# Two encoder layers on one core: measured costs in the planner that places the mixers' steps, a third MLA head at a time, and a different first group

## The chip, the cores and the metric

One core of a Trainium2 chip runs the whole kernel in one launch. The metric is device time in microseconds: the median over several runs, beside one profiled execution from which all rows come. The engines are PE (TensorE), ACT (ScalarE), DVE (VectorE), POOL (GpSimd) and SP (SyncE), which here only issues DMAs.

## The reference, cut to what matters

Two layers, 256 tokens, width 2048, all in float32. Each layer is

```python
h = rms_norm(x, norm_mix)
z = h @ w_in                       # 2048 -> 4304 columns, split over three mixers
y = concat(mlstm(...), mla(...), dilated(...))   # 4, 6 and 6 heads of 128
x = x + y @ w_out
h = rms_norm(x, norm_ff)
x = x + relu(h @ w_ff1) ** 2 @ w_ff2             # 2048 -> 8192 -> 2048
```

The MLA heads (latent attention) take their queries, keys and values from two normed latents of the first columns of z; the dilated heads are attention with a bias of window counts; the mLSTM heads are two directions of a gated linear attention.

## The kernel before, in words

**Products.** A float32 product is three products of float32r parts: hi x hi, hi x lo, lo x hi. Every weight tile (128 x 1024, two contraction tiles of 512 columns) is loaded by SP into one of three buffers `wst`, cast to `whi` by ACT, and DVE takes the rest into `wlo` (`Weights.load`, `split`); four pairs of `whi` and `wlo` exist, and three are made ahead. In the text a unit is one weight tile and its twelve products of 512 columns, w0, w1, ... are the weight tiles in order, and g in a row is the PSUM of such products. Two PSUM banks take a group, one for each tile of 128 tokens, and four banks (`gps`) serve all groups.

**Stages.** A layer's mixers run nine groups of eight units: group 0 (the MLA latents), group 1 (336 columns: key's rotary part, gates, part of dilated v), groups 2 to 4 (mLSTM q and k, v, output gate), 5 to 8 (dilated). Between them come MLA heads, each with a weight tile of its own (`mla_z`), at the places `MLA_AT` = (group, unit). Then come the output projection and four chunks of feed-forward.

**Order.** The program is written by a planner at build time (`Stream`): the main line issues the products, and every evacuation, head or norm is a task, a generator, of which a step is issued when its due time comes. The planner's clock advances by the cost of each product (`mm`), the due time of a step by the cost of what it waits for on ACT, DVE and POOL (`Engine.COST`) plus `MARGIN`. PE takes its instructions in that order, so a step written too early is a wait of PE. `Stream.start` holds back the main line until there is room: a head needs two PSUM banks (`m`), three `t2` tiles and three `half` tiles; while it is held back, steps of other tasks are issued with no products between them. `junk`, `ss` and `xss` are squares and their sums; `nk`, `nkT`, `qrT`, `mla_s`, `sm_e`, `pT`, `oT` are the stations of an MLA head in this order (normed q and k, transposed, rotary part transposed, scores, softmax, transposed, output); `ml_w`, `ml_st`, `ml_h`, `ml_yT` are an mLSTM head's.

**First group.** In the first layer x comes transposed (`xT`, eight loads). `first_xg` splits it on ACT and DVE, and POOL squares it into `acc`, of which two `stat` products make the mean; `token_factor` makes the token factor `rt` of it. x itself (two loads of 1 MB) is loaded after group 1 (`after()`). The latents, `z` and `dv` are read out of PSUM with `rt`.

Of the kernel before, what the change touches and what calls it, by code (L numbers as in the profile page):

```python
# [17 lines left out]
P = 128  # L18
# [48 lines left out]
T2, HALF = 22, 7  # L67

MLA_AT = ((2, 3), (2, 7), (3, 3), (3, 7), (4, 3), (4, 7))
MARGIN = 0.4  # L70


class Engine:
# [3 lines left out]
        "activation": (0.16, 0.00083), "copy": (0.07, 0.00083), "tensor_tensor": (0.07, 0.00104),  # L77
        "scalar_tensor_tensor": (0.13, 0.00104), "tensor_scalar": (0.07, 0.00080), "tensor_copy": (0.07, 0.00104),
        "tensor_reduce": (0.07, 0.00104), "tensor_tensor_reduce": (0.07, 0.00104), "reciprocal": (0.07, 0.0066),
        "tensor_tensor_scan": (0.07, 0.00104), "memset": (0.07, 0.0004),  # L80
    }

# [3 lines left out]
    def __getattr__(self, f):  # L86
# [4 lines left out]
        def call(*args, **kw):  # L91
# [25 lines left out]
class Stream:  # L117
# [98 lines left out]
class Weights:  # L216
# [7 lines left out]
    def load(self):  # L224
# [3 lines left out]
        c.nc.sync.dma_start(self.st[self.d][:, :n], src)  # L228
        self.d += 1

    def split(self):

        c, nc = self.c, self.c.nc
        st, n = self.st.pop(self.k), self.srcs[self.k][1]
# [3 lines left out]
        def parts():  # L238
            nc.scalar.copy(hi[:, :n], st[:, :n])
            yield  # L240
            nc.vector.tensor_tensor(out=lo[:, :n], in0=st[:, :n], in1=hi[:, :n].bitcast(F32), op=ALU.subtract)
# [94 lines left out]
def first_xg(c, xg, kt, src, gain):  # L336
# [11 lines left out]
    c.s.cur.last.pop("pool", None)  # L348
# [987 lines left out]
```

## Time and profile before

| what | us |
|---|---|
| median of 3 runs (2155.4 to 2157.72) | 2156.25 |
| the profiled execution | 2155.49 |
| its span, first to last instruction | 2153.3 |
| PE busy in it | 2119.8 |
| DVE, ACT, POOL busy | 1322.4, 1082.3, 110.4 |

The span lies 2.2 us below the profiled execution's own time. Busy time of PE is modelled at its ends, so a short wait shows shorter than it is.

### The profile page before, as it was taken

How to read it: one execution, taken by the hardware profiler on the slowest of the kernel's cores; microseconds unless marked ns; L12 is line 12 of the kernel's file. 1: busy time of each engine (PE TensorE's matmuls, PEld its weight loads, DVE VectorE, ACT ScalarE, POOL GpSimd, SP SyncE). 2: the span in 40 equal slices, each digit the busy share in tenths (PEclk: the TensorE clock that was granted, in tenths of full speed). 3: DMA queues.
4: the chain of work that ended last, by engine and by line, in shares of the span. 5: the costliest groups of instructions: out<-in, count | busy, mean ns of one | idle time of the engine just before them, and what ended most of it. 6: DMA issues, size and time to landing. Idle time of an engine off the chain costs nothing.

```text
span 2153.3 us, 28894 instructions
## 1 busy us (share of the span) xinstructions
PE 2119.8 (98%) x10848; PEld 1804.9 (84%) x10848; DVE 1322.4 (61%) x1963; ACT 1082.3 (50%) x1883; POOL 110.4 (5%) x142
## 2 busy tenths in 40 slices
PE   8999999999999999999999999999999999999999
PEld 6788888888888888888887888888888888888887
DVE  7668755655564565565557687556546655655654
ACT  5666655543453444454456676554434434534442
POOL 6112100000000000000001121000000000000000
PEclk9999999999999999999999999999999999999999
DMA  7544455566656666566554444556565666566565
GB/s 228 189 141 126 154 175 181 187 194 190 193 186 195 194 188 193 190 192 196 178 174 142 143 128 153 174 189 192 186 198 189 190 191 195 187 195 194 187 200 162
DMA packets 109004, 389.89 MB, mean 181 GB/s; under 512 B 12352, under 2 KB 12480, under 8 KB 108608
## 3 DMA queue, kind: packets, MB, share of 16 engines
q1 hardware_dynamic: 107136, 384.97, 56.6%
q10 hardware_dynamic: 1728, 3.07, 0.4%
q8 instruction: 85, 1.39, 0.3%
q14 instruction: 55, 0.45, 0.1%
HBM read 385.90 MB, written 2.10 MB: 180 GB/s over the span
## 4 chain that ended last, share of the span: by engine, by line
PE 89%; ACT 4%; DVE 3%; POOL 2%; issue 1%; DMA 1%; POOLq 0%; ACTq 0%; DVEq 0%; SPq 0%
PE g L194 84%; ACT junk L98 1%; PE mla_z L194 1%; ACT whi L98 1%; DVE wlo L98 1%; POOL acc L98 1%; PE oT L194 1%; POOL sq L98 1%; DMA wst<-w_in 1%; PE xT L200 0%; PE pT L200 0%; PE dil_s L194 0%; PE mla_s L194 0%; POOL rp L98 0%; ACT dil_z L98 0%
## 5 line engine op out<-in xcount | busy, mean ns | idle before, releaser
L98 DVE TENSOR_TENSOR wlo<-wst,whi 128x1024 fp32r<-128x1024 f32 (+2 forms) x732 | 889.5, 1224 | 317.4 <-ACT whi L98 307.7
L98 ACT CAST whi<-wst 128x1024 fp32r<-128x1024 f32 (+2 forms) x732 | 761.2, 1043 | 539.7 <-PE g L194 402.5
L194 PE MATMUL g<-whi,u 128*128 128x512 f32 x2048 | 633.4, 389 | 0.0
L194 PE MATMUL g<-xg,whi 128*128 128x512 f32 x2048 | 489.8, 391 | 0.0
L194 PEld LDWEIGHTS g<-whi,u 128*128 128x128 f32 x2048 | 384.5, 188 | 79.6
L194 PEld LDWEIGHTS g<-xg,whi 128*128 128x128 f32 x2048 | 376.4, 188 | 72.8
L194 PE MATMUL g<-wlo,u 128*128 128x512 f32 x1024 | 398.4, 389 | 0.0
L194 PE MATMUL g<-whi,xg 128*128 128x512 f32 (+1 forms) x1152 | 371.7, 389 | 6.3 <-ACT whi L98 6.3
L194 PEld LDWEIGHTS g<-xg,wlo 128*128 128x128 f32 x2048 | 263.1, 191 | 12.1 <-ACT xg L98 2.0
L194 PE MATMUL g<-xg,wlo 128*128 128x256 f32 x2048 | 267.4, 283 | 1.1 <-ACT xg L98 1.1
L194 PEld LDWEIGHTS g<-whi,xg 128*128 128x128 f32 x1152 | 215.5, 189 | 44.0 <-ACT whi L98 6.3
L194 PEld LDWEIGHTS g<-wlo,u 128*128 128x128 f32 x1024 | 192.3, 188 | 39.8
L194 PE MATMUL g<-wlo,xg 128*128 128x512 f32 (+1 forms) x576 | 222.0, 385 | 3.3 <-DVE wlo L98 3.3
L98 ACT COPY ev<-g 128x256 f32<-128x256 f32 x128 | 48.0, 375 | 340.7 <-PE g L194 340.7
L98 DVE TENSOR_TENSOR ev<-g,ev 128x256 f32<-128x256 f32 x128 | 54.4, 425 | 229.8 <-ACT ev L98 229.7
L194 PE MATMUL g<-whi,y 128*128 128x512 f32 x512 | 162.8, 393 | 0.0
L194 PEld LDWEIGHTS g<-wlo,xg 128*128 128x128 f32 x576 | 109.1, 189 | 23.3 <-DVE wlo L98 6.7
L194 PEld LDWEIGHTS g<-whi,y 128*128 128x128 f32 x512 | 96.1, 188 | 19.7
L194 PE MATMUL g<-wlo,y 128*128 128x512 f32 x256 | 99.7, 389 | 0.0
L98 DVE SCALAR_TENSOR_TENSOR x<-g,r,x 128x512 f32<-128x512 f32 x64 | 45.8, 751 | 83.2 <-PE g L194 83.2
L98 DVE SCALAR_TENSOR_TENSOR ev<-ev 128x256 f32<-128x256 f32 x128 | 54.4, 425 | 4.4
L194 PEld LDWEIGHTS g<-wlo,y 128*128 128x128 f32 x256 | 48.1, 188 | 9.5
(206 smaller groups left out, 1199.1 us busy)
## 6 DMA issues: line engine op xcount, KB each, us to landing
wst<-w_ff SPq DMA_DIRECT2D x512, 512.0 KB, 4.2
wst<-w_in SPq DMA_DIRECT2D x128, 512.0 KB, 3.7
wst<-w_out SPq DMA_DIRECT2D x64, 512.0 KB, 4.2
wst<-w_in SPq DMA_DIRECT2D x16, 336.0 KB, 3.0
wst<-w_mla SPq DMA_DIRECT2D x12, 416.0 KB, 3.1
xt<-xT SPq DMA_DIRECT2D x8, 256.0 KB, 5.1
x<-x SPq DMA_DIRECT2D x2, 1024.0 KB, 7.1
out<-x ACTq DMA_DIRECT2D x8, 256.0 KB, 2.2
```

Of the source, the lines that this page charges most:

```text
L98: return fn(*args, **kw)
L194: c.nc.tensor.matmul(out, lhsT, rhs, start=start, stop=stop)
```

## The change

Six edits. (1) The planner's cost table gets other numbers: larger fixed parts, POOL at four times DVE's cost by element, an accumulating activation 0.2 more, an engine free 0.08 before an instruction's cost is over; a product of 512 columns counts 0.2266, not 0.2158. (2) `HALF` is 9, not 7, and MLA heads begin at other places. (3) At most two mLSTM heads run at once. (4) The first layer's token factor comes from x itself: eight squares on ACT (`squares`), as every other norm has it; POOL's squares, `acc` and the `stat` products are gone, and the two loads of x stand in the last two units of group 0. (5) Ten float32 products of ones, 128 x 128, stand ahead of everything (`warm_up`); the first `xT` load is on ACT's queue, and the first weight tile is loaded, cast and split in two halves. (6) The very last unit does its six products for the first token tile, then the six for the second.

```diff
-T2, HALF = 22, 7
-
-MLA_AT = ((2, 3), (2, 7), (3, 3), (3, 7), (4, 3), (4, 7))
+T2, HALF = 22, 9
+
+MLA_AT = ((2, 7), (3, 4), (4, 1), (4, 7), (5, 5), (6, 3))
 MARGIN = 0.4
+ML_AT_ONCE = 2
+WARM = 10
...
     COST = {
-        "activation": (0.16, 0.00083), "copy": (0.07, 0.00083), "tensor_tensor": (0.07, 0.00104),
+        "activation": (0.26, 0.00086), "copy": (0.19, 0.00084), "tensor_tensor": (0.155, 0.00105),
...
+    OVERLAP, READ = 0.08, 0.2
...
             if self.name == "pool":
-                fixed, each = 0.15, 2 * each
-            self.s.issue(self.name, fixed + each * n)
+                fixed, each = 0.3, 4 * each
+            elif self.name == "act" and kw.get("accum_out") is not None:
+                fixed += self.READ
+            self.s.issue(self.name, fixed + each * n, self.OVERLAP)
...
-    def issue(self, name, cost):
+    def issue(self, name, cost, overlap):
         last = self.cur.last
         t = max([self.free[name], self.clk] + [v for k, v in last.items() if k != name])
-        self.free[name] = t + cost
+        self.free[name] = t + cost - overlap
...
-    c.s.product(n / 2400.0 * (1 if lhsT.dtype == F32R else 4) + 0.0025)
+    c.s.product(n / 2400.0 + 0.0133 if lhsT.dtype == F32R else n / 1200.0 + 0.0025)
...
+    def pieces(self, i):
+
+        n = self.srcs[i][1]
+        return [slice(0, n // 2), slice(n // 2, n)] if i == 0 else [slice(0, n)]
...
-    if kt == 0:
-        c.acc = c.small.tile([P, S], F32, tag="acc", name="acc", bufs=1)
-        nc.gpsimd.tensor_tensor(out=c.acc, in0=src, in1=src, op=ALU.mult)
-    else:
-        sq = c.tmp.tile([P, S], F32, tag="sq", name="sq", bufs=1)
-        nc.gpsimd.tensor_tensor(out=sq, in0=src, in1=src, op=ALU.mult)
-        nc.gpsimd.tensor_tensor(out=c.acc, in0=c.acc, in1=sq, op=ALU.add)
...
+def squares(c, tt, g, ss):
+
+    j = c.tmp.tile([P, 512], F32, tag="junk5", name="junk5", bufs=1)
+    c.nc.scalar.activation(j, c.x[tt][:, g * 512:(g + 1) * 512], AF.Square, accum_out=ss[:, tt, g:g + 1])
...
+def last_unit(c, acts, ps, w):
+
+    hi, lo = c.w.next()
+    for tt in range(NT):
+        for j in range(2):
...
+    if first:
+        c.xss = new_ss(c)
         for tt in range(NT):
...
+            for g in range(NX):
+                squares(c, tt, g, c.xss)
+            yield
+    yield
+    mean_square(c, v, c.xss)
...
+def warm_up(c):
+
+    ones = c.big.tile([P, P], F32, tag="big", name="ones")
+    c.nc.vector.memset(ones, 1.0)
+    ps = new_bank(c, "warm")
+    for _ in range(WARM):
+        c.nc.tensor.matmul(ps[:, :P], ones, ones, start=True, stop=True)
...
 def ml_head(c, h):
     nc = c.nc
+    yield from c.s.take(t2=2, half=1, ml=1)
...
+        if kp >= KT // 2 - NT:
+            tt = kp - KT // 2 + NT
+            nc.sync.dma_start(c.x[tt], x[tt])
...
+    load_x(nc.scalar)
```

Where this moves instructions, as the two programs have them (line 98 of before is line 104 of the change, 194 is 200, 200 is 206).

First excerpt, ACT in the first layer from the last unit of group 0 on. `rs_a` and `rs_y` are the logarithm and exponent of the token factor, `lat` the latents' squares. Before:

```order
L98 CAST whi<-wst 128x1024 x2
L98 CAST whi<-wst 128x672 x3
L98 ACTIVATE rs_a<-tf_v 128x2
L98 ACTIVATE rs_y_408<-rs_a 128x2
L98 CAST whi<-wst 128x672
L98 ACTIVATE lat,lat_ss<-g,rt 128x384
L98 ACTIVATE lat,lat_ss<-g,rt 128x128
L98 ACTIVATE lat,lat_ss<-g,rt 128x384
L98 ACTIVATE lat,lat_ss<-g,rt 128x128
L98 CAST whi<-wst 128x672 x2
L98 ACTIVATE rs_a<-lat_ss 128x4
L98 ACTIVATE rs_y_476<-rs_a 128x4
```

In the change three casts of 672 columns, four squares of the first token tile, two casts, four squares of the second tile and three casts stand ahead of this piece:

```order
L104 ACTIVATE rs_a<-tf_v 128x2
L104 ACTIVATE rs_y_476<-rs_a 128x2
L104 CAST whi<-wst 128x1024
L104 ACTIVATE lat,lat_ss<-g,rt 128x384
L104 ACTIVATE lat,lat_ss<-g,rt 128x128
L104 ACTIVATE lat,lat_ss<-g,rt 128x384
L104 ACTIVATE lat,lat_ss<-g,rt 128x128
L104 CAST whi<-wst 128x1024
L104 ACTIVATE z_542<-g,rt 128x80 x2
L104 CAST whi<-wst 128x1024
L104 ACTIVATE junk,kr_ss<-z_542 128x64 x2
L104 ACTIVATE dv<-g,rt 128x256 x2
```

The token factor's two activations now come behind the squares and all eight casts of group 1. `z` and `dv`, whose reading gives the PSUM of group 1 free, follow after the latents' squares, and group 2's first product waits for `dv`'s part on DVE.

Second excerpt, PE at the third MLA head of the first layer (`mla_z` is its first product). Before:

```order
L194 MATMUL g<-wlo,xg 128x512
L194 MATMUL g<-whi,xg 128x512
L200 MATMUL nkT<-const,nk 128x128 x4
L200 MATMUL pT<-const,sm_e 128x128 x4
L200 MATMUL qrT<-const,qr 64x128 x2
L194 MATMUL oT<-p_hi,mla_vh 128x256
L194 MATMUL oT<-p_lo,mla_vh 128x256
L194 MATMUL oT<-p_hi,mla_vl 128x256
L194 MATMUL oT<-p_hi,mla_vh 128x256
L194 MATMUL oT<-p_lo,mla_vh 128x256
L194 MATMUL oT<-p_hi,mla_vl 128x256
L194 MATMUL mla_z<-whi,lat_hl 128x192
```

In the change:

```order
L200 MATMUL mla_s<-krh,qrT_sb 128x256
L200 MATMUL mla_s<-krl,qrT_sb 128x256
L200 MATMUL g<-whi,xg 128x512
L200 MATMUL g<-wlo,xg 128x512
L200 MATMUL g<-whi,xg 128x512
L200 MATMUL mla_z<-whi,lat_hl 128x192
L200 MATMUL mla_z<-wlo,lat_hl 128x192
```

Before, nkT of the second head, pT, qrT and oT of others stood without products ahead of the third head's mla_z. Now only three g products stand between another head's mla_s and it.

Third excerpt, PE in the change ahead of the fifth MLA head, in the sixth unit of group 5. Since the third head's mla_s PE has had 21 g products, two ml_h triples and the fourth head's nkT; behind the piece come three more oT, an ml_h triple and mla_z.

```order
L206 MATMUL qrT<-const,qr 64x128 x2
L206 MATMUL pT<-const,sm_e 128x128 x4
L200 MATMUL ml_h<-ml_va,ml_wt 128x129 x3
L200 MATMUL mla_s<-mla_k,mla_q 128x256 x3
L200 MATMUL mla_s<-krh,qrT_sb 128x256
L200 MATMUL mla_s<-krl,qrT_sb 128x256
L200 MATMUL mla_s<-mla_k,mla_q 128x256 x3
L200 MATMUL mla_s<-krh,qrT_sb 128x256
L200 MATMUL mla_s<-krl,qrT_sb 128x256
L200 MATMUL oT<-p_hi,mla_vh 128x256
L200 MATMUL oT<-p_lo,mla_vh 128x256
L200 MATMUL oT<-p_hi,mla_vl 128x256
```

Here, too, steps stand without g products between them: pT and oT of the third head, qrT and mla_s of the fourth. Before, the fifth head's mla_z stood at the end of the fourth unit of group 4.

On SP the first load of x stands behind w10, the second behind w11; before, both stood behind w19 and the first MLA weight.

## Rows read from the trace of the kernel before

**Rows 1.** The page's busy line: us and share of the span, instructions, by engine.

```profile
PE 2119.8 (98%) x10848; PEld 1804.9 (84%) x10848; DVE 1322.4 (61%) x1963; ACT 1082.3 (50%) x1883; POOL 110.4 (5%) x142
```

**Rows 2.** Stretches: length, busy us of each engine, granted clock, DMA share, GB/s.

```profile
6.00:12.00 6.00, 4.96 (x11) 3.59 (x12) 5.91 (x7) 4.82 (x10) 5.59 (x6) 1.00 1.00 372
...
52.00:75.00 23.00, 21.15 (x113) 17.36 (x114) 17.09 (x45) 12.98 (x35) 1.32 (x3) 1.00 0.67 237
75.00:300.00 225.00, 217.06 (x1167) 183.53 (x1166) 163.96 (x361) 148.57 (x405) 32.64 (x36) 0.98 0.46 145
95.00:110.00 15.00, 11.90 (x63) 9.94 (x63) 10.88 (x25) 10.06 (x32) 2.16 (x3) 0.77 0.31 91
300.00:600.00 300.00, 299.44 (x1518) 255.32 (x1517) 175.38 (x215) 140.81 (x188) 0.00 (x0) 1.00 0.60 189
1118.00:1361.00 243.00, 234.38 (x1274) 198.88 (x1274) 178.83 (x403) 161.23 (x442) 34.62 (x39) 0.99 0.46 145
```

**Rows 3.** Timeline of PE: start us, us, instruction, idle before it and its releaser.

```profile
6.34 0.80 PE L194 MATMUL g<-whi,xg 128*128 128x512 f32 x1 [6.34 <-ACT whi L98]
...
10.99 1.05 PE L194 MATMUL g<-whi,xg 128*128 128x512 f32 x2
...
15.10 0.62 PE L194 MATMUL g<-whi,xg 128*128 128x512 f32 x2
15.55 0.39 PE L194 MATMUL g<-wlo,xg 128*128 128x512 f32 x1
...
52.04 0.50 PE L194 MATMUL g<-wlo,xg 128*128 128x512 f32 x1 [0.52 <-DVE wlo L98]
```

**Rows 4.** PE's waits in 1118 to 1361: us in total, times, longest.

```profile
PE pT L200 <- DVE sm_e L98: 2.9, 1, 2.9
PE dqkT L200 <- POOL dil_z L98: 2.2, 2, 1.2
```

**Rows 5.** Timeline of PE at the third MLA head of the first layer.

```profile
96.79 0.28 PE L194 MATMUL mla_s<-krl,qrT_sb 128*128 128x256 f32 x1
...
101.83 1.17 PE L200 MATMUL pT<-const,sm_e 128*128 128x128 f32 x4 [2.46 <-DVE sm_e L98]
...
103.67 0.58 PE L194 MATMUL oT<-p_hi,mla_vh 128*128 128x256 f32 x1 [0.25 <-ACT p_hi L98]
```

**Rows 6.** Groups by shape, DVE and ACT, 60 to 2150: busy us, mean ns.

```profile
L98 DVE TENSOR_TENSOR wlo<-wst,whi 128x1024 fp32r<-128x1024 f32 x693 | 846.6, 1230 | 304.0 <-ACT whi L98 294.5
L98 ACT CAST whi<-wst 128x672 fp32r<-128x672 f32 x8 | 6.1, 758 | 9.6 <-PE g L194 5.7 <-DMA wst<-w_in 3.9
L98 ACT ACTIVATE junk<-x 128x512 f32<-128x512 f32 x24 | 15.1, 629 | 3.8 <-DVE x L98 3.4
```

**Rows 7.** Groups by shape, 0 to 36.

```profile
L98 DVE SCALAR_TENSOR_TENSOR xg<-xt,vec,xg 128x256 fp32r<-128x256 f32 x16 | 13.5, 886 | 4.6 <-ACT xg L98 4.6
L98 DVE TENSOR_TENSOR wlo<-wst,whi 128x1024 fp32r<-128x1024 f32 x8 | 13.3, 1671 | 0.1
```

**Rows 8.** PE's waits in 0 to 75.

```profile
PE g L194 <- DVE wlo L98: 2.7, 6, 0.8
PE ml_aT L200 <- DVE ml_na L98: 1.8, 1, 1.8
```

**Rows 9.** DMA issues, part 6 of the page: KB each, median us to landing.

```profile
x<-x SPq DMA_DIRECT2D x2, 1024.0 KB, 7.1
```

**Rows 10.** Timeline of ACT around group 1 and the loads of x.

```profile
39.01 0.58 ACT L98 ACTIVATE lat<-g,rt 128x384 f32<-128x384 f32 x1 [1.17 <-DVE rt L98]
...
40.73 0.21 ACT L98 ACTIVATION_READ_ACCUMULATOR lat<-g,rt 128x1 f32 x1
...
50.87 0.79 ACT L98 ACTIVATE z<-g,rt 128x80 f32<-128x80 f32 x2
...
63.88 1.05 ACT L98 CAST whi<-wst 128x1024 fp32r<-128x1024 f32 x1 [5.00 <-DMA wst<-w_in]
```

**Rows 11.** Timeline of DVE at the end of the run.

```profile
2148.61 1.43 DVE L98 SCALAR_TENSOR_TENSOR x<-g,r,x 128x512 f32<-128x512 f32 x2 [7.89 <-PE g L194]
```

More of the change, by code (lines that the diff above doesn't have):

```diff
@@ L238, in parts @@
         def parts():
-            nc.scalar.copy(hi[:, :n], st[:, :n])
+            for cols in pieces:
+                nc.scalar.copy(hi[:, cols], st[:, cols])
             yield
-            nc.vector.tensor_tensor(out=lo[:, :n], in0=st[:, :n], in1=hi[:, :n].bitcast(F32), op=ALU.subtract)
+            for cols in pieces:
+                nc.vector.tensor_tensor(out=lo[:, cols], in0=st[:, cols], in1=hi[:, cols].bitcast(F32),
+                                        op=ALU.subtract)
         t = c.s.spawn(parts())
@@ L358, in next_xg @@
     for tt in range(NT):
-        j = c.tmp.tile([P, 512], F32, tag="junk5", name="junk5", bufs=1)
-        nc.scalar.activation(j, c.x[tt][:, g * 512:(g + 1) * 512], AF.Square, accum_out=ss[:, tt, g:g + 1])
+        squares(c, tt, g, ss)
     for half in range(2):
@@ L430, in w_half, with token_factor @@
         part()
-def token_factor(c, rt):
+def token_factor(c, rt, first):
     nc = c.nc
     v = c.small.tile([P, 2], F32, tag="tf_v", name="tf_v")
-    if c.xss is None:
-        ps = yield from bank(c, "stat")
+    if first:
+        c.xss = new_ss(c)
         for tt in range(NT):
-            mm(c, ps[:, 2 * tt:2 * tt + 2], c.acc[:, tt * P:(tt + 1) * P], c.mean[:, :2], True, True)
-        yield
-        nc.vector.tensor_scalar(out=v, in0=ps[:, 0:4:2], scalar1=EPS, scalar2=None, op0=ALU.add)
-        c.s.give(m=1)
-    else:
-        yield
-        mean_square(c, v, c.xss)
+            for g in range(NX):
[3 more added lines that the diff above has]
+    mean_square(c, v, c.xss)
     y = yield from rsqrt(c, v, 2)
@@ L916, in ml_head @@
     nc = c.nc
+    yield from c.s.take(t2=2, half=1, ml=1)
     kk, qq, ql = c.mlqk[h]
-    yield from c.s.take(t2=2, half=1)
     ws = []
@@ L998, in ml_head, with mixers @@
     split(c, c.y[h], tp[:, :S])
-    c.s.give(m=1, t2=1, half=1)
-def mixers(c, prepare, after):
+    c.s.give(m=1, t2=1, half=1, ml=1)
+def mixers(c, prepare, first):
     nc, s = c.nc, c.s
@@ L1014, in mixers @@
     ps = in_group(c, 512, prepare=prepare)
-    tf = s.spawn(token_factor(c, rt))
+    tf = s.spawn(token_factor(c, rt, first))
     lat = s.spawn(latents(c, ps, rt, tf))
@@ L1024, in mixers @@
     s.spawn(ml_gates(c, z1))
-    if after:
-        after()
     def mla0():
@@ L1040, in mixers @@
     ps = in_group(c, 512, hooks(4))
-    og = s.spawn(ml_o(c, ps, rt))
+    s.spawn(ml_o(c, ps, rt))
     for h in range(ML_H):
@@ L1102, in ffn @@
             ps = two_banks(c)
-            token_group(c, us, ps, 512)
+            if last_layer and ch == NCHUNK - 1 and g == NX - 1:
+                token_group(c, us, ps, 512, range(KT // 2 - 1))
+                last_unit(c, us, ps, 512)
+            else:
+                token_group(c, us, ps, 512)
             c.s.spawn(ff2_end(c, ps, g, l, ch, last_layer, nxt))
@@ L1146, in encoder @@
     c = Ctx()
-    c.tc, c.s = tc, Stream(m=4, t2=T2, half=HALF, dil=4)
+    c.tc, c.s = tc, Stream(m=4, t2=T2, half=HALF, dil=4, ml=ML_AT_ONCE)
     c.nc = Engines(c.s, nc)
@@ L1168, in encoder @@
     c.w = Weights(c, weight_order(c, depth))
+    warm_up(c)
     rest = load_vectors(c, 0)
@@ L1201, in encoder @@
     cr = c.cp.tile([P, C_R], F32R, tag="const_r", name="const_rr")
-    for i in range(c.B_ST):
+    load_x(nc.scalar)
+    c.w.load()
+    for i in range(c.B_ST - 1):
         load_x()
@@ L1213, in encoder @@
     cc = lambda o: c.const[:, o:o + P]
-    c.ident, c.mean, c.one, c.triu, c.tril = cc(C_ID), cc(C_MEAN), cc(C_ONE), cc(C_TRIU), cc(C_TRIL)
+    c.ident, c.one, c.triu, c.tril = cc(C_ID), cc(C_ONE), cc(C_TRIU), cc(C_TRIL)
     c.dilb = c.const[:, C_DILB:C_DILB + NT * S].rearrange("p (t s) -> p t s", t=NT)
     c.identr, c.masks, c.sel = cr[:, 0:P], cr[:, P:3 * P], cr[:, 3 * P:3 * P + 64]
-    def load_tokens():
-        for tt in range(NT):
-            nc.sync.dma_start(c.x[tt], x[tt])
     for l in range(depth):
-        mixers(c, prepare if l == 0 else None, load_tokens if l == 0 else None)
+        mixers(c, prepare if l == 0 else None, l == 0)
         out_proj(c)
```

24 lines of the change are left out of this document (16 added, 8 removed).

## The prediction, made before the change had run

> **What bounds the kernel now.** I read the page's busy line first, then the busy time of each engine by stretches, then PE's waits in the stretches that have any, then the places themselves in the timeline.
>
> PE is busy for 2119.8 of 2153.3 us [rows 1], so at most some 33 us are idle, and the question is where. The stretches answer it [rows 2]. In 300 us of output projection and feed-forward PE misses 0.56 us: that kind of work, by far the longer part of the run, is bound by PE's own products, and no placing of steps can help it. In the mixers of the first layer (75 to 300) PE misses 225 - 217.06 = 7.9 us, in those of the second (1118 to 1361) 243 - 234.38 = 8.6 us. [...] So each layer's mixers lose about 8.3 + 3.4 = 11.7 us. The busy figure counts modelled ends, so I add 3 for short waits that it hides (an estimate: some 20 waits, and a product's record outlasts the distance to the next by 0.16, as two products are 0.45 from start to start but 0.62 to their end [rows 3]). The rest is at the start: the first product runs at 6.34, the third group's second one at 52.04 [rows 3].
>
> The biggest single wait of the mixers is pT's for sm_e, the next dqkT's for POOL [rows 4]. The timeline shows what the first is [rows 5]: the third MLA head is due in the stream and finds no room, since two heads hold 6 of 7 `half` tiles, and the first head's remaining steps are written out with no products between them. PE is through with mla_s at 97 and starts pT at 101.83, oT at 103.67. That is the stretch with clock 0.77.
>
> **The mixers.** Room for nine `half` tiles lets three heads run, and the new places put heads five or six units apart, not four. So the third head follows three products after another head's mla_s (second excerpt): its wait is gone. But two mLSTM heads now hold a `half` each when the fifth MLA head is due (third excerpt), 3 + 3 + 2 = 8 of 9, so that head must wait for the third to end, and steps stand there without products again. I walk it with the distances of [rows 5]. Before: mla_s to pT 4.9 us, pT to oT 1.8. Now PE has 21 g products of 0.225 [rows 3], 4.7 us, and besides two ml_h triples and nkT between mla_s and pT: that covers 4.9. Between pT and oT stand an ml_h triple and a whole mla_s (ten products of half the columns, 1.1): 1.6 to 1.8, just enough. But the softmax steps queue on DVE behind a reciprocal of ml_og and a wlo (1.23 [rows 6]), so I put 1.5 us of waiting there, and no fall of the clock. Bounds: 0, if all is covered; 13 as in rival 4. Saved: 3.1 idle (15 - 11.90 [rows 2]) + 3.4 clock - 1.5 = 5.0 us a layer.
>
> The other waits (11.7 - 6.5 = 5.2, with the hidden 3 about 8 us a layer) are steps that PE meets too early, as dqkT on POOL, 2.2 [rows 4]. The new table charges POOL four times DVE's cost by element, not twice, and the fixed parts of DVE and ACT at about twice the old; a product is charged 0.2266, near what the trace shows, not 0.2158. Steps of such chains therefore stand later. I take half of the 8, 4 us; bounds 1 (waits only change places, as DVE and ACT have the same work to do) and 6. No operation is added to the mixers, and DVE stays below PE (178.8 of 243 [rows 2]). Both layers have the same order after the first head: 2 x 9 = 18 us.
>
> **The start.** Removed: 31 squares and sums on POOL and two stat products. While POOL worked, a wlo took 1.67 us and a gain 0.89 [rows 7], against 1.23 for wlo later [rows 6]; DVE set a pace of 1.67 + 2 x 0.89 = 3.4 us a unit against PE's 12 x 0.225 = 2.7, and PE waited 2.7 for wlo [rows 8]. Without POOL a unit costs DVE some 2.5 by wlo's ratio (an estimate): PE sets the pace. The first weight in halves lets the first product start some 0.5 earlier, near 5.8 (half of a cast; 672 columns take 0.76 [rows 6]). Then 8 x 2.7 and 1.5 of first-unit waits end group 0 near 29, group 1 (96 products, 336/512 of 0.225 each, 14.2, an estimate) near 45, with 1 us of waits as ACT holds its casts behind squares.
>
> But group 2 needs PSUM that only z and dv give free, and these need rt, now made from x itself. SP's order is w10, x, w11, x, w12. A load waits until DVE has finished with the buffer three units back, so the second x goes out after wlo of w8, near 26. It shares the queue with w10, w11 and the first x, 2.8 MB; at 372 GB/s (DMA share 1.00 [rows 2]) that is 7.5 us, the landing of today's x loads being 7.1 [rows 9]: it lands at 34. Then on ACT w12's cast 0.76 and four squares of 0.63 with their reads, 3.0 [rows 6]: 38. Reduction, three casts, logarithm and exponent, DVE's factor: rt near 42. Behind it, in ACT's order (first excerpt): latent squares 1.9, a cast 1.05, z 0.8, a cast [rows 10], k's squares and dv 1.7 (an estimate after z), dv on DVE 0.5: group 2 begins at 49. PE has been idle since 45.
>
> A fall of the clock there is a cost. Before pT 2.5 us without products were followed by 0.77 over 15 us [rows 2]; 1.8 before ml_aT [rows 8] were not, the clock of 52 to 75 being 1.00. So I charge 3 us, 4 us being longer than 2.5. Equivalent start of group 2: 52. Before it began at 52.04 - 0.52 - 0.39 = 51.1, lost 0.5 to wlo [rows 3] and 1.8 at ml_aT, because the x loads held back a weight (ACT waited 5.0 [rows 10]); these loads are over by now. 51.1 + 0.5 + 1.8 - 52 = **1.4 us** gained. Bounds: -4 (second x three to four us later, passed on one for one, and the fall) to +6 (no fall, x at 31).
>
> Ten warm-up products on ones run while data load. Until 12.3 two products took 1.05, then 0.62 [rows 3], so at most some 12 x 0.2 = 2.4 us come early. I count nothing for them: PE would only reach the end of group 1 sooner and wait longer for rt. The cover is that 4 us wait; with x landing 4 us sooner they are worth 2.4.
>
> [...]
>
> **The end.** The last unit does all of token tile 0 first. DVE's two final additions (1.43 together, begun before the last product [rows 11]) end with one that needs that product. Only the first output's transfer moves: 0.2 us (0 to 0.6).
>
> **Sum.** 18 + 1.4 + 0.2 = 19.6. The profiled execution took 2155.49 (span 2153.3); less 19.6 it is 2135.9, and the median of the runs lies 0.8 above the profiled one: 2136.7. I say 2136.5 for the median.
>
> **Rivals.**
> 1. Deeper: x lands early enough that PE does not idle (start +6, the warm-up's 2.4 among them), and the clump costs nothing while three quarters of the short waits go: 2 x (6.5 + 6) + 6 = 31, 2125; short of that anything down from 2129. For it: DVE is free of POOL. Against: x cannot leave SP before w10.
> 2. Waits change places: in the fifth head's clump PE idles 3 us and the clock falls as now, and the short waits keep 7 of 8. Each layer saves 1 to 3, the start 1.4: 2151. For it: two layers show that 2.5 to 2.9 us suffice for a fall [rows 4, 5]. Against: the products counted above.
> 3. No effect: what the start gains the wait for rt returns, and the mixers as in 2 with nothing saved: 2152 to 2160.
> 4. Slower: the clump is exposed whole. If the third head's softmax, its split and the fourth head's nkT, gains and qrT follow each other with nothing between (4.9 + 1.8 from [rows 5], about 3 for the gains and qrT, as an estimate) and the clock falls (3.4), a layer pays 13 there against 6.5 now: +6.5, less 4 for the other waits; with the start at its lower bound, +4, the sum is +9: 2165. It decides where the clump costs more than 6.5 + 4 + 1 = 11.5 a layer. Against: PE's queue holds as much work there as the chain lasts.
>
> **How the numbers follow.** Chances: forecast (2129 to 2145) 0.58, rival 1 (below 2129) 0.14, rival 2 (2145 to 2152) 0.17, rival 3 0.07, rival 4 0.04. 0.2%, about what a measurement of this kernel can tell from no change, is 4.3 us. Faster: 0.58 + 0.14 + 0.17 = 0.89; same 0.07; slower 0.04. The range takes most of rival 1 and rival 2 up to 2150: 2119 to 2150.
>
> **What would show it.** Right: no clock of 0.5 near the third head in either layer; under 2 us of waiting before the fifth head's mla_z; dqkT's wait on POOL gone; wlo at 1.23 from the start; x landed by 35; an idle stretch of 3 to 5 us before group 2 with a fall of the clock behind it; no wait at ml_aT. I am wrong if the fifth head's clump halves the clock, if the second x lands after 38, or if DVE, with mLSTM, MLA and dilated heads together in groups 6 to 8, makes g wait for wlo.

## The result, and the profile after the change

The changed kernel takes 2168.79 us (median of 4 runs, 2168.25 to 2169.46) against 2156.98 for the kernel before in the same comparison: ratio 1.0057, 95% interval 1.0044 to 1.007. The forecast was 2136.5 with a range of 2119 to 2150: wrong in sign, by 32 us.

The page's busy line of the changed kernel answers to [rows 1]:

```profile
PE 2127.2 (98%) x10864; PEld 1809.9 (84%) x10864; DVE 1311.4 (61%) x1966; ACT 1089.2 (50%) x1900; POOL 72.8 (3%) x111
```

PE's idle time has grown from 33.5 to 40.1 us of a span of 2167.3. The products of ones, which do no work of the layers, count as 4.6 us of busy time (the row of `warm` further down), so without them PE's idle time has grown by 11 us. Where, the same stretches tell that stand in [rows 2] (length, busy us of PE, PEld, DVE, ACT and POOL, granted clock, DMA share, GB/s):

```profile
52.00:75.00 23.00, 21.95 (x95) 18.09 (x96) 14.55 (x38) 10.41 (x23) 2.20 (x3) 0.87 0.43 133
75.00:300.00 225.00, 211.92 (x1156) 178.06 (x1156) 161.67 (x363) 149.99 (x418) 26.39 (x36) 1.00 0.45 141
95.00:110.00 15.00, 13.46 (x74) 11.27 (x73) 10.14 (x20) 9.49 (x30) 3.01 (x4) 1.00 0.41 135
...
1118.00:1361.00 243.00, 228.99 (x1227) 193.16 (x1226) 169.24 (x379) 157.02 (x430) 29.57 (x39) 0.98 0.46 142
```

Feed-forward is as before (PE is busy for 299.44 us from 300 to 600 in both). The stretch 95 to 110, where the third MLA head stood, has its clock back (1.00, before 0.77) and PE's busy time has risen from 11.90 to 13.46; the clock is 1.00 in the whole of the first layer's mixers. The third head's wait and its fall of the clock are gone, as forecast. But over the mixers as a whole PE misses 225 - 211.92 = 13.1 us in the first layer (before 7.9) and 243 - 228.99 = 14.0 in the second (before 8.6), and the clock of 52 to 75 has fallen to 0.87.

**Second layer.** PE's waits in the mixers, their total, count and longest, answer to [rows 4]:

```profile
PE g L200 <- DVE wlo L104: 4.2, 4, 1.4
PE ml_w L200 <- DVE y L104: 3.4, 2, 3.3
...
PE pT L206 <- DVE sm_e L104: 0.7, 1, 0.7
```

pT's wait for sm_e is 0.7 us, not 2.9, and dqkT no longer waits for POOL (it waits 0.9 us for DVE). In their place stand many waits for DVE, the longest that of ml_w, an mLSTM head's first products: 3.3 us, where its longest was 1.0 before. Three stretches show the clock of the two places in the second layer and of the start:

```profile
49.00:60.00 11.00, 6.95 (x20) 5.54 (x21) 7.31 (x27) 6.43 (x18) 0.00 (x0) 0.69 0.49 146
1252.00:1262.00 10.00, 8.29 (x31) 6.13 (x30) 7.38 (x13) 4.91 (x9) 0.46 (x1) 0.83 0.53 154
1276.00:1290.00 14.00, 10.74 (x40) 8.26 (x39) 8.30 (x18) 7.26 (x25) 1.97 (x3) 0.76 0.40 128
```

At 0.69, 0.83 and 0.76 the clock is short by 11 x 0.31 = 3.4, 10 x 0.17 = 1.7 and 14 x 0.24 = 3.4 us. Part of this lies within the waits: in steps of 1 us the clock is at its lower level, 0.50, from 51.2 to 58.0, from 1256.0 to 1259.5 and from 1280.0 to 1286.8, while PE's products begin again at 53.05 and 1280.77 in the first and the third. Beside its waits PE loses about 2.5, 1.7 and 3.0 us. PE's timeline at the fifth MLA head and at ml_w, in brackets the idle time before a row and who ended it:

```profile
1241.61 0.72 PE L206 MATMUL pT<-const,sm_e 128*128 128x128 f32 x4 [0.67 <-DVE sm_e L104]
1243.61 0.61 PE L200 MATMUL mla_s<-mla_k,mla_q 128*128 128x256 f32 x3 [0.37 <-DVE qrT_sb L104]
...
1246.78 0.36 PE L200 MATMUL mla_z<-whi,lat_hl 128*128 128x192 f32 x1 [0.35 <-DVE y L104]
...
1253.68 0.50 PE L200 MATMUL g<-wlo,xg 128*128 128x512 f32 x1 [0.96 <-DVE wlo L104]
...
1255.17 0.63 PE L206 MATMUL pT<-const,sm_e 128*128 128x128 f32 x4 [0.76 <-DVE ml_hs L104]
...
1275.39 0.44 PE L206 MATMUL ml_yT<-const,ml_hs 128*128 128x128 f32 x2 [0.85 <-ACT nk L104]
...
1280.77 0.69 PE L200 MATMUL ml_w<-ml_ahl,const_rr 128*128 128x384 f32 x1 [3.26 <-DVE y L104]
```

Before the fifth head's mla_z and behind it PE waits 0.67 + 0.37 + 0.35 + 0.96 + 0.76 = 3.1 us, each wait short, and then the clock falls (1252 to 1262). Twenty us later ml_yT waits 0.85 and ml_w 3.26, and it falls again. What DVE does ahead of the y for which ml_w waits:

```profile
1266.45 0.42 DVE L104 TENSOR_TENSOR y<-oT,y 128x256 fp32r<-128x256 f32 x1 [2.81 <-ACT y L104]
...
1278.12 1.21 DVE L104 TENSOR_TENSOR wlo<-wst,whi 128x1024 fp32r<-128x1024 f32 x1
1279.26 0.28 DVE L104 CAST mla_vh<-mla_z 128x128 fp32r<-128x128 f32 x1
...
1280.30 0.41 DVE L104 TENSOR_TENSOR y<-ml_yT,y 128x256 fp32r<-128x256 f32 x1
...
1285.10 0.42 DVE L104 TENSOR_TENSOR y<-ml_yT,y 128x256 fp32r<-128x256 f32 x1 [3.25 <-ACT y L104]
```

ml_w needs the PSUM that y gives free. The product under y, ml_yT, ran at 1275.39; y's DVE half is written behind a weight's wlo and the casts of the sixth MLA head's v, and DVE comes to it 4.9 us later. DVE has no idle time just there: from 1266.45 to 1281.85 its instructions follow each other almost without a gap. But it has stood 2.81 us before that stretch and stands 3.25 us behind it, each time for ACT's half of a y; over 1276 to 1290 it is busy for 8.30 of 14 us (third of the three stretches). So DVE has time enough, loses it in waits for ACT, and what PE needs first comes last in its queue.

**The start.** The page's row of the loads of x answers to [rows 9]:

```profile
x<-x SPq DMA_DIRECT2D x2, 1024.0 KB, 6.3
```

The row gives the middle of the two: the first load took 5.1 us, the second 7.5. Issued at 28.9, the second lands near 36.4 (forecast 34). ACT's timeline around the token factor answers to [rows 10]:

```profile
33.10 0.63 ACT L104 ACTIVATE junk<-x 128x512 f32<-128x512 f32 x1 [1.67 <-DMA x<-x]
...
43.33 0.20 ACT L104 ACTIVATE rs_a<-tf_v 128x2 f32<-128x2 f32 x1
...
46.30 1.05 ACT L104 CAST whi<-wst 128x1024 fp32r<-128x1024 f32 x1 [2.54 <-DMA wst<-w_in]
```

The eight squares run from 33.1 to 40.9, with casts between them that wait for weights, and rt is there near 45 (forecast 42). Then ACT stands before a weight's cast that waits 2.54 us for its DMA, ahead of the latents' squares. Between 20 and 48 us a weight takes 5.4 us at the median from issue to landing, in the kernel before 3.2; the two loads of x, 2 MB, now go through the same queue in that time. PE's first product of group 2:

```profile
53.05 0.80 PE L200 MATMUL g<-whi,xg 128*128 128x512 f32 x1 [4.86 <-DVE dv L104]
```

PE has waited 4.86 us, and about 2.5 us of lost clock follow.

Without POOL's squares a wlo on DVE takes the forecast 1.23 us, answering to [rows 7] (groups by shape, 0 to 36):

```profile
L104 DVE TENSOR_TENSOR wlo<-wst,whi 128x1024 fp32r<-128x1024 f32 x7 | 8.7, 1236 | 4.7 <-ACT whi L104 4.6
```

So group 1 ended earlier, and the wait for rt took it back. At the first feed-forward unit, from which on both kernels run the same products with next to no waits, the change is 5.6 us behind (380.1 against 374.5 on PE's timeline), at the last product 14.1 (2162.98 against 2148.86): 8.5 us come from the second layer's mixers, which have no part in the new start, and 5.6 from the start and the first layer's.

### The profile page after: what moved, and what is told of

Read it like the earlier page. It is cut to its first block, busy times and chain, and to the rows that moved or that the text cites. A ratio compares the mean times of both kernels' runs of the same rounds, so it can differ in the third digit from the quotient of the medians.

```text
span 2167.3 us, 28883 instructions
## 1 busy us (share of the span) xinstructions
PE 2127.2 (98%) x10864; PEld 1809.9 (84%) x10864; DVE 1311.4 (61%) x1966; ACT 1089.2 (50%) x1900; POOL 72.8 (3%) x111
## 4 chain that ended last, share of the span: by engine, by line
PE 90%; ACT 4%; DVE 3%; DMA 2%; issue 1%; SPq 0%; ACTq 0%; DVEq 0%
PE g L200 85%; DMA wst<-w_in 2%; DVE wlo L104 1%; ACT junk L104 1%; ACT whi L104 1%; PE mla_z L200 1%; PE oT L200 1%; PE xT L206 0%; PE mla_s L200 0%; PE pT L206 0%; PE dil_s L200 0%; PE ml_w L200 0%; PE ml_h L200 0%; PE dqkT L206 0%; ACT ml_wt L104 0%
## 5 line engine op out<-in xcount | busy, mean ns | idle before, releaser
L200 PE MATMUL g<-whi,xg 128*128 128x512 f32 (+1 forms) x1152 | 378.9, 394 | 6.4 <-DVE dv L104 4.9
```

The costliest lines, as they stand in the source:

```text
L200: c.nc.tensor.matmul(out, lhsT, rhs, start=start, stop=stop)
```

## The experiments

The edits are those of the change by number: (1) the planner's numbers, (2) room (`HALF`) and places (`MLA_AT`), (3) the limit on mLSTM heads, (4) to (6) start and end. Each kernel is compared with the kernel before run beside it (medians 2155.8 to 2156.9); what stands in brackets is the interval of the ratio.

### One edit of the change undone

`old_costs` takes the hunks of `Engine` and `mm` back:

```diff
...
-    OVERLAP, READ = 0.08, 0.2
...
-                fixed, each = 0.3, 4 * each
...
+                fixed, each = 0.15, 2 * each
...
-    c.s.product(n / 2400.0 + 0.0133 if lhsT.dtype == F32R else n / 1200.0 + 0.0025)
+    c.s.product(n / 2400.0 * (1 if lhsT.dtype == F32R else 4) + 0.0025)
```

> The changed kernel with the planner's old numbers (cost table, no overlap, no read, 0.2158 a product); places, room, limit and start as changed. Theory A (places: MLA heads in groups 5 and 6 now stand beside the mLSTM heads and the first dilated pair, ACT and DVE serve all of them in order, and PE meets their steps late): little comes back, 2165 to 2172. Theory B (costs: the larger numbers write steps later, heads overlap longer and pile up in groups 5 to 7): the ml_w wait of 3.3 us and its fall of the clock go in both layers, 2150 to 2158.

Measured 2176.37, ratio 1.0096 (1.0081 to 1.0111): 7.6 us slower still than the change.

`old_places` takes the places and the room back and lifts the limit:

```diff
-T2, HALF = 22, 9
+T2, HALF = 22, 7
-MLA_AT = ((2, 7), (3, 4), (4, 1), (4, 7), (5, 5), (6, 3))
+MLA_AT = ((2, 3), (2, 7), (3, 3), (3, 7), (4, 3), (4, 7))
...
-ML_AT_ONCE = 2
+ML_AT_ONCE = 4
```

> The changed kernel with the old places, HALF 7 and no limit on mLSTM heads; new costs, new start. Theory A (places): the waits of groups 5 to 7 go, the third head's clump with its fall of the clock comes back, 2150 to 2158, in the second layer's mixers about 20 us of lateness as before. Theory B (costs): the waits stay or grow beside the old clump, 2166 to 2175.

Measured 2177.52, 1.01 (1.0085 to 1.0115): 8.7 slower than the change. Both theories had expected that one of these two would come back to the old time. Neither did: numbers and places each lose, alone more than together. (old_places gives up the room and the limit as well; the runs below take these apart.)

`old_start` is the kernel before with edits (1) to (3); its one line that is in neither kernel lets POOL's scratch square share a buffer with a later one of ACT, so that nine `half` tiles fit:

```diff
-        sq = c.tmp.tile([P, S], F32, tag="sq", name="sq", bufs=1)
+        sq = c.tmp.tile([P, 512], F32, tag="junk5", name="sq", bufs=1)[:, :S]
```

> The kernel before with the new costs, places, room and limit: the first group with POOL's squares, x after group 1, no warm-up, old last unit (POOL's scratch square shares a buffer with a later one of ACT, so that nine half tiles fit). By the landmarks of the two traces the start is worth nothing (change about 0.3 us later at the third group's fifth unit, one MLA head taken off): 2167 to 2170. If the wait for the token factor (5 us and a fall of the clock) is a loss of its own, 2163 or less.

Measured 2165.89, 1.0045 (1.0028 to 1.0061): the new start and end cost 2.9 us, between the two cases. The intervals of this ratio and of the change's overlap, so a cost of this size is only just told from none.

`no_limit` changes one number:

```diff
-ML_AT_ONCE = 2
+ML_AT_ONCE = 4
```

> The changed kernel with four mLSTM heads allowed at once. Theory A (places): with the limit gone the mLSTM heads compete with the fifth MLA head for half tiles, 2166 to 2174. Theory C (limit: it pushes the third and fourth mLSTM head among the dilated ones, and their ml_w waits for the first two heads' end): the ml_w wait of 3.3 us and its fall of the clock go in both layers, 2155 to 2160.

Measured 2174.13, 1.0084 (1.0069 to 1.0099). The limit gains 5.3 us; without it the wait moves from ml_w to a head's nkT, which waits 4.0 us for the same kind of y.

### Room alone, the fifth head's place, the time of x

`room9` is the kernel before with `T2, HALF = 22, 9`, and the shared square of `old_start`.

> The kernel before with HALF 9 in place of 7 (POOL's scratch square shares a buffer with a later one of ACT to make room); places, costs, start and limit as before. Theory E (room alone was the cause of the third head's clump): its idle time and fall of the clock go, some 6 us a layer, and the rest stays: 2142 to 2148. Theory F (three heads at once bring steps that meet each other in group 5, as in the changed kernel): new waits of the same size, 2152 to 2160.

Measured 2145.94, 0.9947 (0.9931 to 0.9964): 10 us faster than before. Theory E holds. The room is the part of the change that does what the forecast said.

`room9_newcosts` is the changed kernel with the old places, no limit and `HALF = 9`.

> The changed kernel with the old places and no limit, but HALF 9: against room9 the new costs and the new start. The start costs 2.9 us by the run without it. If the new costs are worth something once no head is held back, below room9 + 2.9; if they are worse in themselves (every forced wait of the main line issues more steps with no products between), room9 + 2.9 + 5 to 18.

Measured 2183.68, 1.0124 (1.0109 to 1.0139). Against room9 and the start's 2.9 the numbers cost 35 us. `no_limit` is this kernel with the new places and took 2174.13: beside the new numbers the new places gain 9.6 us.

`fifth_later` moves two heads:

```diff
-MLA_AT = ((2, 7), (3, 4), (4, 1), (4, 7), (5, 5), (6, 3))
+MLA_AT = ((2, 7), (3, 4), (4, 1), (4, 7), (5, 7), (6, 5))
```

> The changed kernel with the fifth and sixth MLA heads two units later, (5, 7) and (6, 5). Theory G (the clump ahead of the fifth head, held back for room, makes ACT and DVE late, and the wlo, pT, ml_yT and ml_w waits of the next 35 us with their falls of the clock follow from it): the clump is spread over two more units, and these waits shrink by half or more: 2155 to 2162. Theory D (crowding: six MLA heads' ends, four mLSTM heads and the dilated heads stand in groups 5 to 8 whatever the unit): the waits only move, 2166 to 2178.

Measured 2169.8, 1.006 (1.0045 to 1.0075): as the change. PE's waits moved, to dqkT (3.8 us for a y of DVE) and others. Theory D, not G: my picture of the fifth head's clump as the source of what follows fell here.

`x_early` moves the two loads:

```diff
-        if kp >= KT // 2 - NT:
-            tt = kp - KT // 2 + NT
+        if 4 <= kp < 4 + NT:
+            tt = kp - 4
```

> The changed kernel with the two loads of x at units 4 and 5 of group 0, not 6 and 7. If the late x is what holds up the third group, x lands some 8 us sooner, the wait of 5 us before that group and its fall of the clock (3.4) go, and weights are late by at most 2 x 2.8: 2160 to 2166. If the weights' delay takes all of it, 2167 to 2171.

Measured 2168.33, 1.0053 (1.0038 to 1.0068): no change. The loads left SP at 21.1 and 24.2 in place of 28.0 and 28.9, and ACT's timeline still had this:

```profile
32.90 0.75 ACT L104 CAST whi<-wst 128x672 fp32r<-128x672 f32 x1 [2.57 <-DMA wst<-w_in]
33.56 0.63 ACT L104 ACTIVATE junk<-x 128x512 f32<-128x512 f32 x1
...
42.88 0.20 ACT L104 ACTIVATE rs_a<-tf_v 128x2 f32<-128x2 f32 x1
...
46.16 1.05 ACT L104 CAST whi<-wst 128x1024 fp32r<-128x1024 f32 x1 [2.85 <-DMA wst<-w_in]
```

The squares begin 0.5 us later than in the change, rs_a 0.4 sooner, the cast of 46.16 at the same time. The place of x's loads is not what holds up group 2: the squares stand in ACT's order behind casts that wait for weights (the one of 32.90 for 2.57), and behind rt the cast of 46.16 waits for its own. Whether these weights would come sooner with no load of x in the queue at all, no run tells. The step in the forecast that let rt follow from x's landing was wrong.

### Which number

Four edits of room9, each alone. `room9_product` has the new cost of a product, `room9_table` the new table, `OVERLAP` and `READ`, `room9_pool` POOL's line, `room9_limit` the limit:

```diff
-    c.s.product(n / 2400.0 * (1 if lhsT.dtype == F32R else 4) + 0.0025)
+    c.s.product(n / 2400.0 + 0.0133 if lhsT.dtype == F32R else n / 1200.0 + 0.0025)
```

> room9 (2145.9) with the product's cost of 0.2266 alone. room9 with all new numbers and the new start took 2183.7, of which the start is 2.9, so the numbers together are worth +35 there. A larger product makes the planner's clock run faster for each product, so steps are written after fewer products. Theory H (this is the part that hurts, steps met too early): 2152 to 2170. Theory I (the engines' numbers do it): 2143 to 2149.

Measured 2149.49, 0.9969 (0.9956 to 0.9981): +3.6 against room9, with intervals that overlap.

```diff
-        "activation": (0.16, 0.00083), "copy": (0.07, 0.00083), "tensor_tensor": (0.07, 0.00104),
+        "activation": (0.26, 0.00086), "copy": (0.19, 0.00084), "tensor_tensor": (0.155, 0.00105),
...
+    OVERLAP, READ = 0.08, 0.2
```

> room9 with the new numbers of ACT and DVE alone (table, overlap, read of an accumulating activation); POOL and product as before. Theory I (with longer chains the heads finish later, so mLSTM, MLA and dilated steps stand together in groups 5 to 7, and the forced waits of the main line issue more steps with no products between): 2155 to 2180. Theory H: 2140 to 2149, a little better even, as steps are written later.

Measured 2193.14, 1.0167 (1.0152 to 1.0183): +47 against room9, the largest effect of all. Theory I.

```diff
-                fixed, each = 0.15, 2 * each
+                fixed, each = 0.3, 4 * each
```

> room9 with POOL at 0.3 and four times DVE's cost by element alone. POOL's rope steps take 0.46 to 0.76 for 128 columns here and are charged 0.84. Theory J (POOL's number holds back k's rotary part, so that the first MLA head's forced wait takes ml_At with it, and each head's qr comes later): 2150 to 2165. If POOL's number only mends dqkT's wait as the prediction had it: 2143 to 2147.

Measured 2158.44, 1.0009 (1.0 to 1.0019): +12.5. dqkT's wait for POOL is gone, as the forecast had it, but in the second layer ml_At now waits 1.6 us for DVE, as theory J lets one expect, and wlo is waited for 5.7 us. The three together cost 35 us (room9_newcosts), less than their sum.

```diff
+ML_AT_ONCE = 2
...
-    yield from c.s.take(t2=2, half=1)
+    yield from c.s.take(t2=2, half=1, ml=1)
```

> room9 with at most two mLSTM heads at once. In the changed kernel the limit is worth 5.3 us (without it 2174.1 against 2168.8). If that holds here, since DVE in groups 5 and 6 has less to do at a time: 2138 to 2144. If the limit only pushes the last two mLSTM heads among the dilated heads: 2148 to 2158.

Measured 2138.28, 0.9914 (0.9899 to 0.9929): -7.7, and 18 us faster than the kernel before. In its second layer PE waits in two places only (why the limit helps was not followed further):

```profile
PE g L195 <- DVE wlo L99: 2.1, 2, 1.4
PE dqkT L201 <- POOL dil_z L99: 1.0, 2, 0.9
```

### What the table and the places do

`only_places` is room9_limit with the new `MLA_AT`, one line.

> room9_limit (2138.3) with the new places alone: old costs, old start, HALF 9, limit 2. By subtraction (old_costs 2176.4 less the start's 2.9) 2173.5, so that the new places alone cost 35 us: 2171 to 2176. If start and places meet in the first layer, 2160 to 2170.

Measured 2173.76, 1.0073 (1.0056 to 1.009): the places alone cost 35 us. So the whole change is a ladder of single steps: room -10, limit -7.7, places +35.5, numbers -7.9, start and end +2.9; their sum is the change's 12 to within 1. Its fourth step has the other sign than on the old places: with heads begun late the new numbers mend a little of what the places lose. So numbers and places each cost 35 us without the other, and each gains 8 to 10 us where the other already stands. The fourth corner, new numbers with old places under the limit, was not run.

What the places do, a stretch of 60 us shows that begins 160 us into the second layer, room9_limit first (columns as in the stretches above):

```profile
1234.98:1294.98 60.00, 59.75 (x328) 51.01 (x327) 49.59 (x115) 40.92 (x122) 11.77 (x12) 1.00 0.48 145
```

The same and the next 60 us of only_places:

```profile
1253.21:1313.21 60.00, 54.80 (x288) 45.50 (x288) 39.04 (x104) 39.79 (x136) 8.35 (x11) 0.94 0.36 113
1313.21:1373.21 60.00, 55.64 (x293) 46.16 (x293) 46.16 (x108) 40.18 (x101) 8.00 (x6) 1.00 0.45 133
```

DVE is busy for 49.59 us in the one and 39.04 in the other, and the 60 us after that are the busier ones (46.16): heads begun later do their work later, among the dilated heads. (PE itself gets through 288 products there and not 328, so a part of DVE's difference is only that everything is late.) There DVE and ACT meet in a way that the timeline of only_places shows best. DVE:

```profile
1316.87 0.48 DVE L99 SCALAR_TENSOR_TENSOR mla_q<-nkT,vec,mla_q 128x256 fp32r<-128x256 f32 x1 [5.85 <-ACT mla_k L99]
...
1319.11 1.22 DVE L99 TENSOR_TENSOR wlo<-wst,whi 128x1024 fp32r<-128x1024 f32 x1
```

ACT, the first of eight squares and the step whose end DVE waits for:

```profile
1310.74 0.30 ACT L99 ACTIVATE junk<-dil_z 128x128 f32<-128x128 f32 x1
...
1316.38 0.46 ACT L99 ACTIVATE mla_k<-nkT,vec 128x256 fp32r<-128x256 f32 x1
```

PE:

```profile
1320.38 0.50 PE L195 MATMUL g<-wlo,xg 128*128 128x512 f32 x1 [3.27 <-DVE wlo L99]
```

DVE stands 5.85 us before mla_q, whose first half ACT has still to make: on ACT eight squares of dilated heads, a weight's cast and a softmax stand ahead of it. The wlo of the next weight, which needs nothing of mla_q, stands on DVE behind it and seven other rows and begins at 1319.11, and PE waits 3.27 us for it. DVE has idle time there, 5.85 us, in which none of the eight rows behind mla_q runs. This is the longest of PE's waits for wlo in that layer; together they are the largest in only_places, against 2.1 us in room9_limit:

```profile
PE g L195 <- DVE wlo L99: 8.2, 6, 3.3
```

One place is followed here; that all 35 us come about in this way is not shown.

`table_margin0` and `table_vh` ask why the table loses:

```diff
-MARGIN = 0.4
+MARGIN = 0.0
```

> room9_table (2193.1) with MARGIN 0 in place of 0.4, which takes up to 0.4 off the due time at each station of a chain. Theory K (the table hurts because due times come too late: DVE and ACT work of groups 2 to 4 slips into groups 5 to 8 and later): most comes back, 2150 to 2170. Theory L (it hurts by where single steps stand in DVE's and ACT's own order, splits behind steps that wait for the other engine): 2180 to 2200.

Measured 2159.7, 1.0012 (1.0003 to 1.0022): 33 of the 47 us come back. A smaller margin might help without the table, too; room9 with no margin was not run. But in room9 PE is busy for 220.17 of 225 us (75 to 300) and 237.32 of 243 (1118 to 1361), with a clock of 1.00 and 0.99 there, so its mixers have only some 13 us to give back (4.8 + 5.7, and 2.4 of clock). Most of the 33 hangs on the table.

```diff
+    yield
     vh = c.half.tile([P, NT, MLA_V], F32R, tag="half", name="mla_vh")
```

> room9_table with one more yield in the MLA head: the cast and rest of v on DVE are a step of their own, behind the six squares on ACT, not in one step with them. In room9_table DVE waits 22.1 us in the second layer's mixers at these casts for ACT's squares, with wlo, and so SP's loads, behind it. Theory L: these waits go, and with them wlo's 4 to 6 us a layer and some falls of the clock: 2165 to 2182. Theory K: no more than 3 us, 2188 to 2195.

Measured 2177.52, 1.0093 (1.0078 to 1.0108): 15.6 come back, as theory L said and more than K allows. Each theory's own test came out as it had it: both are at work. 33.4 + 15.6 = 49.0 is more than 47.2 by less than the noise, so whether they overlap is open; no run has both edits. The row that table_vh was made for, on DVE in room9_table:

```profile
1240.45 0.29 DVE L102 CAST mla_vh<-mla_z 128x128 fp32r<-128x128 f32 x1 [3.77 <-ACT junk L102]
...
1242.13 2.35 DVE L102 TENSOR_TENSOR wlo<-wst,whi 128x1024 fp32r<-128x1024 f32 x2
```

DVE stands 3.77 us before the casts of v, with two wlo behind them; for the first of these PE waits 1.50 us. And the lateness as a whole, by stretches of 60 us that begin 40 and 280 us into the second layer (counted from the last product of the first layer's feed-forward, on PE's timeline at 1077.24, 1102.80 and 1083.63). room9:

```profile
1117.24:1177.24 60.00, 58.15 (x306) 48.18 (x305) 41.34 (x97) 39.78 (x109) 6.57 (x9) 0.97 0.51 160
1357.24:1417.24 60.00, 60.00 (x276) 49.63 (x275) 33.14 (x37) 29.84 (x44) 0.00 (x0) 1.00 0.61 191
```

room9_table:

```profile
1142.80:1202.80 60.00, 53.35 (x268) 45.33 (x269) 34.18 (x82) 35.65 (x100) 5.70 (x9) 0.91 0.43 136
1382.80:1442.80 60.00, 60.00 (x292) 50.35 (x291) 38.79 (x59) 31.77 (x53) 0.00 (x0) 1.00 0.58 179
```

table_margin0:

```profile
1123.63:1183.63 60.00, 57.44 (x300) 48.20 (x299) 41.43 (x96) 39.60 (x109) 6.79 (x9) 0.97 0.50 156
1363.63:1423.63 60.00, 60.00 (x281) 49.88 (x281) 33.39 (x38) 28.07 (x41) 0.00 (x0) 1.00 0.59 190
```

With the table DVE does 34.18 us of work in the first stretch, not 41.34, and 38.79 in the last, when the mixers should be over, not 33.14. (Here, too, PE gets through fewer products in the first stretch, 268 and not 306.) With no margin both are back (41.43 and 33.39). The larger numbers came on top of a margin of 0.4 at each station of a chain.

`after_margin0` is the changed kernel with `MARGIN = 0.0`.

> The changed kernel with MARGIN 0. With the old places the table's loss shrank from 47 to 14 us by this. Theory K (late due times are a large part of the changed kernel's loss): 2140 to 2155. If with the new places it is the places alone that hold it up (35 us with the old numbers, which write steps earlier): 2165 to 2180.

Measured 2155.79, 0.9996 (0.9986 to 1.0005): 13 us better than the change, and even with the kernel before, in the range of theory K. Late due times account for that much of the change itself, unless a smaller margin gains by itself, which here no run rules out.

### Two more versions

`best` is room9_limit with the first weight in halves, the first xT on ACT's queue and the new last unit.

> room9_limit (2138.3) with the edits of the start that do not touch the token factor, and the last unit: the first weight in halves, the first xT on ACT's queue, the last unit's products by token tile. No warm-up. The first product starts at about 5.8 in place of 6.3, and the end gains 0.2: 2136.5 to 2138.3.

Measured 2140.26, 0.9923 (0.9908 to 0.9938): not up to 2 us faster, but 2 slower, with intervals that overlap: nothing gained. Its first product starts at 7.00, in room9_limit at 6.43.

`limit_vh` is room9_limit with the `yield` of table_vh.

> room9_limit (2138.3) with the casts of v as a step of their own. With the table this gave 15.6 us; here DVE waits 10.1 us at these casts in the second layer's mixers, but PE loses only two waits of over 1 us there, one of them for wlo (1.7): 2134 to 2139 if that wait and its like in the first layer go, 2139 to 2146 if other steps stand later for it.

Measured 2139.74, 0.9927 (0.9912 to 0.9941): nothing gained, though 15.6 were with the table. The fastest version remains room9_limit, two ideas of the change out of many.

## Why the prediction was wrong

**The step that failed** is the pair of prices in "The mixers". The new places stand in the sum with 1.5 us a layer at the fifth head and nothing else; the new numbers stand in it with a gain of 4 us a layer, since the new table lets steps "therefore stand later". Together they were to gain 8 - 3 = 5 us. They cost 27.6: 2165.89 with both (old_start) against 2138.28 without (room9_limit). That is the miss of 32 us; the other terms, room, limit, start and end, were off by +3, -7.7 and +4.5 us, which cancel.

**The numbers:** "I take half of the 8, 4 us; bounds 1 ... and 6". I took later for safer. On the old places the table alone is +47 us, POOL's line +12.5 and the product +3.6, so there even the sign of the lower bound was wrong. Its reason, that DVE and ACT have the same work to do and DVE stays below PE, is true (169.24 us of 243 in the second layer, 178.83 before) and does not help: the question is not how much work DVE has but what stands ahead of a wlo in its queue when ACT is late (in only_places mla_q, with 5.85 us of waiting, ahead of the wlo of 1319.11). In the change itself the numbers gain 7.6 us (old_costs), near the 8 of the forecast. That is luck: as far as the runs go, they gain only beside heads begun late, a condition that the forecast did not set.

**The places** were costed by the room that heads need, at nothing otherwise. With the old numbers they are +35 us; in the place followed above, late heads' steps meet the dilated heads' squares on ACT. I named this as a way to be wrong ("with mLSTM, MLA and dilated heads together in groups 6 to 8, makes g wait for wlo") and gave it neither a price nor a rival. The limit, too, stood at nothing and is worth 5 to 8 us.

**The third head:** right in its mechanism. Room alone gives 10 us. The figure to set beside it is 2 x (3.1 + 3.4) = 13, since the 1.5 taken off for the fifth head belong to the new places, which room9 does not have. The 3.4 is, by the stretch 95 to 110 in [rows 2], 15 us x 0.23, and the trace shows as much in both layers: in steps of 1 us the clock of the kernel before is at 0.50 for 6.8 us from 101.1 on and for 6.8 us from 1169.5 on. Some 0.5 us of each 3.4 was counted twice, as PE is busy for only some 5.7 of the 6.8. And room9 has short waits of its own, 1.9 us of ml_yT in the second layer.

**The fifth head's clump:** mis-sized. Forecast 1.5 us and no fall of the clock; measured 1.4 us of waiting before mla_z and 1.7 behind it, with 1.7 of clock in the second layer and none in the first. It is under half of what rival 4 needed, so the loss did not come that way: fifth_later moved it and gained nothing.

**The start:** forecast a gain of 1.4 (-4 to +6), measured a loss of 2.9 with the end. wlo at 1.23, no wait at ml_aT, the idle time before group 2 and the fall behind it (3 charged, some 2.5 measured) were right. The second x came 2.4 us later than counted. Group 2 began at 53.05, not 49, because of casts in ACT's order that wait for weights, which I had counted as lasting only as long as they run. The first product began at 7.19, not near 5.8: halving the first weight gains nothing while ACT's first step, which stands ahead of its cast, waits for an xT that now comes through ACT's own queue. That step began at 4.09 before and begins at 5.72 now:

```profile
5.72 0.91 ACT L104 ACTIVATE xg<-xt,vec 128x256 fp32r<-128x256 f32 x2 [3.71 <-DMA xt<-xT]
```

**The warm-up:** the forecast counted nothing, and it gave nothing, but not for the reason given. PE's timeline at the start, to be read beside [rows 3]:

```profile
1.05 4.63 PE L488 MATMUL warm<-ones 128*128 128x128 f32 x20 [1.05 <-DVE ones L104]
7.19 0.79 PE L200 MATMUL g<-whi,xg 128*128 128x512 f32 x1 [1.51 <-ACT whi L104]
...
12.35 1.05 PE L200 MATMUL g<-whi,xg 128*128 128x512 f32 x2
...
13.63 0.63 PE L200 MATMUL g<-whi,xg 128*128 128x512 f32 x2
```

The products of ones run from 1.05 to 5.68. The products behind them still take 1.05 for two at 12.35, and 0.63 only from 13.63, 6.4 us after the first at 7.19; before, the first shorter pair (0.68) starts at 12.27, 5.9 after the first product at 6.34. Two other kernels without products of ones lie on either side: 4.8 us in room9_limit (a pair of 0.76 at 11.18, the first product at 6.43) and 7.6 in best (0.67 at 14.64, the first at 7.00). So in this trace the products of ones do not bring the shorter times forward; the 2.4 us that the prediction set as their most was an estimate, and no run shows any of it. What decides when the shorter times begin stays open.

**Chances:** "slower" had 0.04. All cases but one took the new numbers for a help of some size, and none gave the places a price beyond the clump. The rows of the kernel before show the work of the steps, not what a later place for them costs.

## What to carry to other kernels

A planner's costs and its safety margin belong together: where the costs are raised towards the measured ones, the margin that made up for the low ones has to be set again, or chains are written late (here 33 of 47 us). Two ideas that each look safe can cost 35 us each and not add up, so a price for one holds only beside a stated setting of the other. And where, as on DVE here, rows stand behind one that waits (5.85 us before mla_q, then 3.27 us of PE for the wlo behind it), ask of every moved step what stands behind it, for whom, and whether its other half can be late on another engine; an engine with a quarter of its time free can still be the one that PE waits for most (DVE in the second layer's mixers of the change: busy for 169.24 of 243 us). A change of several ideas is best taken apart before it is judged: here two of them give 18 us, and the rest hid that.

## What the runs showed of the hardware

In these runs the length of a wait did not by itself tell whether the granted clock fell behind it. In the second layer of the change five waits of no more than 1 us each (0.67, 0.37, 0.35, 0.96 and 0.76 between 1241 and 1256) were followed by the lower level (0.50 from 1256.0 to 1259.5, a mean of 0.83 over 1252 to 1262), and ml_w's wait of 3.26 by another fall (0.76 over 1276 to 1290). In its first layer the same steps stand in the same order and wait as long (0.66, 0.38, 0.34, 0.95 and 0.75 between 168 and 183, then 3.12 before ml_w), and the clock is 1.00 over the whole of 75 to 300:

```profile
180.70 0.50 PE L200 MATMUL g<-wlo,xg 128*128 128x512 f32 x1 [0.95 <-DVE wlo L104]
...
206.20 0.44 PE L200 MATMUL ml_w<-ml_ahl,const_rr 128*128 128x384 f32 x1 [3.12 <-DVE y L104]
```

Nor did it fall behind a single wait of 3.27 at 1320 in only_places: the stretch 1313 to 1373 shows 1.00. The prediction had gone by the length of single waits, 2.5 to 2.9 us as enough for a fall; what decides it no run here tells.
